# Four products that nobody reads behind each of the steps 8 to 26 of the recurrence

## The chip, the cores and the metric

The kernel runs on one core of a Trainium2 chip. A core has five engines that work side by side, each through a queue of its own in a fixed order: TensorE (PE in the profile; PEld is its loading of weights), VectorE (DVE), ScalarE (ACT), GpSimd (POOL) and SyncE (SP), which here issues nearly all DMA transfers. TensorE writes into PSUM, eight banks of 128 x 512 floats; VectorE and ScalarE read them out. Engines wait for one another by semaphores. The metric is the device time of one execution in microseconds (us), the median of several runs. [...]

## The reference

Two layers of a streaming encoder on 256 tokens of width 2048, all in float32. Layer 0 mixes tokens by causal pooling, layer 1 by RWKV-7; a SwiGLU block with a hidden width of 5632 follows each. The part that matters is the recurrence of layer 1, for 32 heads of size 64:

```python
def step(state, inp):
    r_t, w_t, k_t, v_t, a_t, b_t = inp
    sa = jnp.einsum('bhvk,bhk->bhv', state, a_t)
    state = (state * w_t[:, :, None, :] + sa[..., None] * b_t[:, :, None, :]
             + v_t[..., None] * k_t[:, :, None, :])
    return state, jnp.einsum('bhvk,bhk->bhv', state, r_t)
...
_, y = lax.scan(step, state0, seq_in)
...
return (y * g) @ w_o
```

## The kernel before, in words

Every float32 product of a large matrix is made of three products of a shorter float format (fp32r): ScalarE rounds a weight tile (`wh`, line 152), VectorE takes the rest (`wl`, line 153), and TensorE multiplies both. The stages follow one another: the pooling layer, the SwiGLU block (`ffn`, lines 311 to 347), the RWKV layer (`rwkv`), the second SwiGLU block.

The recurrence isn't stepped token by token. The 256 tokens are cut into four chunks of 64, and the 32 heads into eight groups of four (`gi`). For each group `ready(gi)` loads two tiles `KB` and `AR` that an earlier stage has put into DRAM (lines 832, 833), transposes them (L840), multiplies them (L853), masks the result into `G` (VectorE, L856), and completes the inverse of a small triangular system `Z` (L875, L882). `chains(gi)` then goes through the four chunks, three steps each, 12 steps for a group. A step is a few small float32 products of 64 or 128 rows and a copy out of PSUM: L907 and L910 into `cb`, then ScalarE's copy `rhs` (L912); L916, then the copy into `vt` or `sv` (L917); L921 and L925, then VectorE's update of the state `S` (L930, L932) and ScalarE's `Se` and `y` (L936, L937). A new group begins every 8 steps (`STAG`), so that one or two groups are under way; `all_chains` counts 68 steps in all.

`weave` puts the other work of this stage between the steps: `invert(1)` inverts the systems of groups 4 to 7 by 31 rounds of two VectorE instructions (`sysP`, L633, and `sysZ`, L634) on a tile `sysM` that four DMAs load (L624) out of `dM`, which the last of the `prepare` steps has written (L607); `head_norm` normalises a finished group (ScalarE's `ysq` L980 and a square root L990, VectorE's L976 to L996), where a DMA L973 brings a row of weights into a place that the group before must have left; `gating` (L958 to L960) multiplies `hid` by a loaded tile; `out_proj` (L1022 to L1024) multiplies finished groups by the output weights with 512 columns a product.

The program names the work in this order, and a scheduler sorts it by priorities (the chains' are raised) and by when it thinks that operands are there; the order on each engine is fixed when the program is built. PSUM banks come from three pools: three for `acc`, three for `g` (`g_bank`, used by `ready`, `head_norm`, `gating` and, until it ends, `prepare`), two for `cb`. A bank is given out in rotation and is waited for until its last reader is done. `queued(name)` keeps an instruction behind another on the same engine.

Of the kernel before, what the change touches and what calls it, by code (L numbers as in the profile page):

```python
# [40 lines left out]
LASTO = 6  # L41
OA, OB = 0, 0
STAG, OG, RE = 8, 2, 0
BANKS = {"acc": 3, "g": 3, "cb": 2}
DECAY = float(np.exp(-0.5))

# [46 lines left out]
def hybrid_encoder(ctx: ExitStack, tc: tile.TileContext, I, out):  # L93
    nc = tc.nc
# [5 lines left out]
    base = cp.tile([128, 5120], F32, name="base")  # L100
# [34 lines left out]
    last = {}  # L135

    def queued(name):
        return tc.issue_after(last[name].ins)
# [111 lines left out]
    def ffn(layer, each=None):  # L250
        gcol = par[f"g2_{layer}"]
        with ExitStack() as st:
# [1 line left out]
            ff = st.enter_context(tc.tile_pool(name="ff", bufs=1))  # L254
            tps = st.enter_context(tc.tile_pool(name="ftp", bufs=1, space=PSUM))
            ps = st.enter_context(tc.tile_pool(name="fps", bufs=1, space=PSUM))
            rb = base[:, 4864:]
            xs = []
            xs_ = ff.tile([128, KT * 512], F32R, name="xs")
            for k in range(KT):  # L260
# [189 lines left out]
    def rwkv():  # L450
        with ExitStack() as st:
# [3 lines left out]
            def mx(dt, name="mx"):  # L455
                return lp.tile([128, 512], dt, name=name, tag="mx", bufs=MX)
# [23 lines left out]
            hid = [hid_[:, q * 512:(q + 1) * 512] for q in range(4)]  # L480
# [16 lines left out]
            def bank(tag, bufs):  # L497
                return ps[tag].tile([128, 512], F32, name=tag, tag=tag, bufs=bufs)

            acc_bank = lambda: bank("acc", BANKS["acc"])  # L500
            g_bank = lambda: bank("g", BANKS["g"])
            cb_bank = lambda: bank("cb", BANKS["cb"])

# [383 lines left out]
            def chains(gi):  # L887

                vt, z, S = vts[gi], Z[gi % 3], Sb[gi % 2]
                ar_, kbt_, g_ = AR[gi], KBT[gi], G[gi]  # L890
                y = ys_raw[gi] = mx(F32, "y")

                sv = (vt, c2.tile([128, 512], F32, name="sv", tag="sv", bufs=3))
                nc.gpsimd.tensor_copy(sv[1][kh[1]], vt[kh[1]])
                odd[gi] = sv[1]
                heads_ = [(jj, slice(hd * 64, hd * 64 + 64), jj * 2 + hd) for jj in range(2) for hd in range(2)]
                Se = None
                for c in range(4):
                    q, i = c % 2, c // 2
                    k_, b_ = kh[q], kh[1 - q]  # L900
                    vrow = sv[q][:, i * 256:(i + 1) * 256]
                    rows_of = lambda u: vrow[:, u * 64:(u + 1) * 64]
                    two = lambda x: x.rearrange("p (j c) -> p j c", j=2)
                    with tc.high_priority(HP):
                        cb = cb_bank().rearrange("p (j x c) -> p j x c", j=2, x=2)
                        for jj, hc, u in heads_:
                            nc.tensor.matmul(cb[:, jj, 0, hc], lhsT=g_[jj][u % 2][k_, c], rhs=rows_of(u)[k_], start=(u == 0), stop=False, skip_group_check=True)  # L907
                        if c:
                            for jj in range(2):
                                nc.tensor.matmul(cb[:, jj, 0], lhsT=ar_[jj][:, c], rhs=S[c % 2][:, jj], start=False, stop=False, skip_group_check=True)  # L910
                        rhs = c2.tile([128, 2, 128], F32, name="rhs", tag="rhs", bufs=2)
                        nc.scalar.copy(rhs[b_], cb[b_, :, 0])  # L912
                    yield
                    with tc.high_priority(HP):
                        for jj, hc, u in heads_:
                            nc.tensor.matmul(cb[b_, jj, 1, hc], lhsT=z[b_, u * 2 + i], rhs=rhs[b_, jj, hc], start=True, stop=True, skip_group_check=True)  # L916
                        nc.scalar.copy(two(vrow[b_]), cb[b_, :, 1])  # L917
                    yield
                    with tc.high_priority(HP):
                        for jj, hc, u in heads_:  # L920
                            nc.tensor.matmul(cb[k_, jj, 0, hc], lhsT=g_[jj][u % 2][b_, c, k_], rhs=rows_of(u)[b_], start=False, stop=True, skip_group_check=True)  # L921
                        if c < 3:
                            up = cb[:, :, 1]
                            for jj, hc, u in heads_:
                                nc.tensor.matmul(up[hc, jj, :64], lhsT=kbt_[jj][:, c, hc], rhs=rows_of(u), start=True, stop=True, skip_group_check=True)  # L925
                            S2 = S[1 - c % 2]
                            for jj, hc, u in heads_:
                                e_ = ends[hc, gi * 2 + jj, c:c + 1]
                                if c:
                                    nc.vector.scalar_tensor_tensor(S2[hc, jj, hc], up[hc, jj, :64], e_, Se[hc, jj, hc], ALU.mult, ALU.add)  # L930
                                else:
                                    nc.vector.tensor_scalar(S2[hc, jj, hc], up[hc, jj, :64], e_, None, ALU.mult)  # L932
                            if c < 2:
                                Se = c2.tile([128, 2, 128], F32, name="Se", tag="Se", bufs=2)
                                for jj in range(2):
                                    nc.scalar.activation(Se[:, jj], S2[:, jj], AF.Copy, scale=ends[:, gi * 2 + jj, c + 1:c + 2])  # L936
                        nc.scalar.copy(two(y[k_, i * 256:(i + 1) * 256]), cb[k_, :, 0])  # L937
                    yield

            def all_chains():  # L940

                live = []
                for step in range(7 * STAG + 12):
                    if step % STAG == 0 and step < 8 * STAG:
                        live.append(chains(step // STAG))
                    live = [g for g in live if next(g, g) is not g]
                    yield

            def gating(gi):
# [132 lines left out]
            E_ = 7 * STAG + 12  # L1082
            more += [(last_weights(), 4, E_ - 12, E_ - 2), (head_norm(7, 0, 1), 4, E_ - 5, E_)]
            weave(all_chains(), *more)
            outs = chained(*rest)
            for _ in head_norm(7, 1, 2):
# [5 lines left out]

    pool_layer()
    ffn(0)
    rwkv()
    if True:
        def times_gain(n, fgB):
            with queued("load"):
                nc.sync.dma_start(fgB, I["rows"][3, n * 512:(n + 1) * 512].partition_broadcast(128))
            for i in range(2):  # L1100
                nc.vector.tensor_mul(h[i][n], h[i][n], fgB)

        ffn(1, times_gain)
        rstd = rstd_of_h()
        for n in range(4):
            for i in range(2):
                o = h[i][n]
                if i:
                    nc.scalar.activation(o, o, AF.Copy, scale=rstd[:, i:i + 1])
                else:  # L1110
                    nc.vector.tensor_scalar(o, o, rstd[:, i:i + 1], None, ALU.mult)
                (nc.sync if i else nc.scalar).dma_start(out[i * 128:(i + 1) * 128, n * 512:(n + 1) * 512], o)
# [53 lines left out]
```

## Time and profile before

| what | value |
|---|---|
| median of 3 runs | 2181.81 us (2181.44 to 2184.13) |
| the profiled execution, its own time | 2181.9 us |
| its span, first to last instruction | 2180.1 us |
| TensorE busy | 2116.9 us, 97% of the span |
| TensorE's weight loads busy | 1843.5 us, 85% |
| VectorE busy | 1553.9 us, 71% |
| ScalarE busy | 1147.3 us, 53% |
| mean granted TensorE clock | 0.981 |

A busy share is an average over all stages. The row of the clock cuts the span into 40 slices of 54.5 us. In a timeline a row is one instruction or a run of like ones: its start, how long it took, and in brackets how long its engine had stood idle before it and who ended that. The matmuls of a run overlap, so their pace is read from one start to the next. A float32 matmul of the program appears in the trace as two.

### The profile page before, as it was taken

To read this page: it belongs to the slowest core of one execution; us is meant where nothing else is said; L and a number is where in the kernel's file an instruction comes from. 1 tells how busy PE (TensorE), PEld (TensorE's weight loads), DVE (VectorE), ACT (ScalarE), POOL (GpSimd) and SP (SyncE) were. 2 spreads that over 40 slices of the span, in tenths; PEclk is the share of its full clock that TensorE was granted. 3 is DMA by queue.
4 is the path that set the end of the run, shared out by engine and by line. 5 is a ranking of instruction groups with operands and counts; after the bars stand their busy time and mean duration, and the time that the engine had idled before them with its cause. 6 is when DMAs were issued, how large, how long until landed. Compare 5 with 4: busy or idle time off the path is not lost.

```text
span 2180.1 us, 34748 instructions
## 1 busy us (share of the span) xinstructions
PE 2116.9 (97%) x13318; PEld 1843.5 (85%) x13318; DVE 1553.9 (71%) x2548; ACT 1147.3 (53%) x1884; POOL 30.6 (1%) x72
## 2 busy tenths in 40 slices
PE   7999999999999989999999999999999999999997
PEld 5888888888878879999988778788888888888786
DVE  8666666666787978688866767876666666677886
ACT  5544444444555478766745354554444444445444
POOL 0000000000000000011000000000000000000000
PEclk9999999999999999999998699999999999999999
DMA  6555565665566645466565343446666666655654
GB/s 232 174 187 191 186 191 187 190 187 190 196 198 217 207 155 163 163 210 207 171 218 151 108 121 105 160 121 191 188 189 189 188 189 189 188 191 199 204 202 156
DMA packets 147478, 395.11 MB, mean 181 GB/s; under 512 B 39280, under 2 KB 46832, under 8 KB 147056
## 3 DMA queue, kind: packets, MB, share of 16 engines
q1 hardware_dynamic: 146160, 390.80, 56.2%
q8 instruction: 104, 1.70, 0.3%
q10 hardware_dynamic: 1152, 2.10, 0.3%
q14 instruction: 62, 0.51, 0.1%
HBM read 376.59 MB, written 16.25 MB: 180 GB/s over the span
## 4 chain that ended last, share of the span: by engine, by line
PE 86%; DVE 6%; DMA 4%; ACT 2%; issue 1%; SPq 0%; ACTq 0%; DVEq 0%
PE acc L311 29%; PE acc L347 17%; PE acc L313 15%; PE acc L691 2%; PE acc L689 2%; PE acc L690 2%; DVE wl L153 2%; PE tp L347 2%; PE acc L1022 1%; PE acc L1024 1%; PE acc L1023 1%; DMA raw<-in_w 1%; PE acc L516 1%; PE acc L515 1%; PE cb L907 1%
## 5 line engine op out<-in xcount | busy, mean ns | idle before, releaser
L153 DVE TENSOR_TENSOR wl<-raw,wh 128x1024 fp32r<-128x1024 f32 (+1 forms) x525 | 640.2, 1220 | 432.2 <-ACT wh L152 428.0
L152 ACT CAST wh<-raw 128x1024 fp32r<-128x1024 f32 (+1 forms) x525 | 548.5, 1045 | 648.7 <-PE acc L311 276.9
L311 PE MATMUL acc<-xs,wh 128*128 128x512 f32 x2816 | 710.6, 393 | 3.7 <-DVE xs L266 3.2
L311 PEld LDWEIGHTS acc<-xs,wh 128*128 128x128 f32 x2816 | 504.9, 189 | 94.9 <-DVE xs L266 5.1
L313 PEld LDWEIGHTS acc<-xs,wl 128*128 128x128 f32 x2816 | 384.1, 190 | 27.5
L313 PE MATMUL acc<-xs,wl 128*128 128x256 f32 x2816 | 392.7, 282 | 0.0
L347 PE MATMUL acc<-vh,gT 128*128 128x512 f32 x640 | 184.9, 390 | 0.8 <-ACT vh L152 0.8
L347 PEld LDWEIGHTS acc<-vh,gT 128*128 128x128 f32 x640 | 119.7, 188 | 27.3 <-ACT vh L152 2.6
L691 PE MATMUL acc<-mx,wl 128*128 128x256 f32 x464 | 133.0, 287 | 3.5 <-DVE wl L153 3.5
L689 PE MATMUL acc<-mx,wh 128*128 128x256 f32 x464 | 132.1, 285 | 0.0
L690 PE MATMUL acc<-mx,wh 128*128 128x256 f32 x464 | 131.8, 284 | 0.0
L153 DVE TENSOR_TENSOR vl<-raw,vh 128x1024 fp32r<-128x1024 f32 x80 | 95.5, 1221 | 27.1 <-ACT vh L152 19.7
L347 PE MATMUL acc<-vl,gT 128*128 128x512 f32 x320 | 112.2, 389 | 0.0
L152 ACT CAST vh<-raw 128x1024 fp32r<-128x1024 f32 x80 | 80.9, 1050 | 49.3 <-PE acc L347 22.7
L355 ACT CAST vh<-T 128x1024 fp32r<-128x1024 f32 x56 | 58.9, 1052 | 80.5 <-DVE T L397 43.6
L347 PE MATMUL acc<-wh,gT 128*128 128x512 f32 x320 | 93.8, 390 | 0.7 <-ACT wh L152 0.7
L691 PEld LDWEIGHTS acc<-mx,wl 128*128 128x128 f32 x464 | 88.5, 191 | 5.3 <-DVE wl L153 5.2
L689 PEld LDWEIGHTS acc<-mx,wh 128*128 128x128 f32 x464 | 88.5, 191 | 0.8
L690 PEld LDWEIGHTS acc<-mx,wh 128*128 128x128 f32 x464 | 88.6, 191 | 0.0
L347 PE MATMUL acc<-vh,g 128*128 128x512 f32 x280 | 77.9, 391 | 1.1 <-ACT vh L355 0.6
L516 PE MATMUL acc<-wl,mx 128*128 128x256 f32 x256 | 74.2, 290 | 1.2 <-DVE wl L153 1.1
L515 PE MATMUL acc<-wh,mx 128*128 128x256 f32 x256 | 74.2, 290 | 0.0
(329 smaller groups left out, 3118.5 us busy)
## 6 DMA issues: line engine op xcount, KB each, us to landing
raw<-in_w SPq DMA_DIRECT2D x528, 512.0 KB, 4.4
raw<-in_wk SPq DMA_DIRECT2D x32, 512.0 KB, 3.7
raw<-in_wr SPq DMA_DIRECT2D x32, 512.0 KB, 3.7
raw<-in_wv SPq DMA_DIRECT2D x32, 512.0 KB, 4.0
raw<-in_wo SPq DMA_DIRECT2D x32, 512.0 KB, 3.6
raw<-in_pw SPq DMA_DIRECT2D x8, 512.0 KB, 7.8
dKB<-KB SPq DMA_DIRECT2D x16, 256.0 KB, 3.1
dKB<-AR SPq DMA_DIRECT2D x16, 256.0 KB, 3.7
```

Source lines behind the costliest of these rows:

```text
L152: nc.scalar.copy(wh[:P, :step], raw[:P, :step])
L153: nc.vector.tensor_sub(wl[:P, :step], raw[:P, :step], wh[:P, :step].bitcast(F32))
L311: nc.tensor.matmul(acc, lhsT=w[:, cs], rhs=xs[q * 4 + kk], start=(q + kk == 0), stop=False, skip_group_check=True)
L313: nc.tensor.matmul(acc[:, :256], lhsT=l[:, cs], rhs=xs[q * 4 + kk][:, :256], start=False, stop=(q + kk == 6), skip_group_check=True)
L347: nc.tensor.matmul(out_, lhsT=lhsT, rhs=rhs, start=start, stop=stop, skip_group_check=True)
L355: nc.scalar.copy(wh, src)
L515: nc.tensor.matmul(av[:, i], lhsT=xh, rhs=w[:, cs], start=(k == 0 and i == 0), stop=False, skip_group_check=True)
L516: nc.tensor.matmul(av[:, i], lhsT=xh, rhs=l[:, cs], start=False, stop=False, skip_group_check=True)
L689: nc.tensor.matmul(acc[:, :256], lhsT=w[:, cs], rhs=xs[k][:, :256], start=(k == 0), stop=False)
L690: nc.tensor.matmul(acc[:, :256], lhsT=w[:, cs], rhs=xs[k][:, 256:], start=False, stop=False)
L691: nc.tensor.matmul(acc[:, :256], lhsT=l[:, cs], rhs=xs[k][:, :256], start=False, stop=(k == 15))
L907: nc.tensor.matmul(cb[:, jj, 0, hc], lhsT=g_[jj][u % 2][k_, c], rhs=rows_of(u)[k_], start=(u == 0), stop=False, skip_group_check=True)
```

## The change

`idle_products` takes a bank of the `g` pool and multiplies four times a 128 x 128 part of `hid[2]` by the 512 columns of `hid[3]` into it. Nothing reads the bank. `all_chains` calls it once behind each of the steps 8 to 26, 19 times, so that 76 products come in. Each is queued behind the last of the chains' L907, L916 or L921 that stands before it in the program. The slice of `base` in `ffn` names its end now; the tile has that width anyway.

```diff
+IDLE0, IDLE1, IDLES = 8, 27, 4
...
-            rb = base[:, 4864:]
+            rb = base[:, 4864:5120]
...
-                            nc.tensor.matmul(cb[:, jj, 0, hc], lhsT=g_[jj][u % 2][k_, c], rhs=rows_of(u)[k_], ...)
+                            last["chain"] = nc.tensor.matmul(cb[:, jj, 0, hc], lhsT=g_[jj][u % 2][k_, c], rhs=rows_of(u)[k_], ...)
...
+            def idle_products():
+
+                acc = g_bank()
+                for _ in range(IDLES):
+                    with queued("chain"):
+                        nc.tensor.matmul(acc, lhsT=hid[2][:, :128], rhs=hid[3], start=True, stop=True, skip_group_check=True)
+
             def all_chains():
...
                     live = [g for g in live if next(g, g) is not g]
+                    if IDLE0 <= step < IDLE1:
+                        idle_products()
                     yield
```

The scheduler sorts the whole stage anew. Line numbers grow by 1 from line 44 on and by 10 behind `idle_products`. On TensorE the order ahead of the first new product is the old one, and so is that behind the end of the RWKV layer; in between much has changed its place.

Three places follow. The first is TensorE at the first new products, in `ready` of group 2: `KB_12332` is the first `KB` tile of that group and `KB_12460` the second (in the new program `KB_12337` and `KB_12475`). Before:

```order
L853 MATMUL g_12405<-AR_12333,KB_12332 128x128 x4
L907 MATMUL cb_12521<-sv_12321,base_64 128x64 x4
L910 MATMUL cb_12521<-S_11276,AR_11800 128x128
L910 MATMUL cb_12521<-S_11276,AR_11952 128x128
L853 MATMUL g_12406<-AR_12333,KB_12332 128x128 x4
L907 MATMUL cb_12687<-vt_10845,base_64 128x64 x4
L840 MATMUL g_12465<-base_64,KB_12460 128x128 x4
L853 MATMUL g_12547<-AR_12461,KB_12460 128x128 x2
L916 MATMUL cb_12521<-rhs_12528,Z1_11271 64x64 x4
```

Now, where L946 is the new product:

```order
L946 MATMUL g_12410<-hid_6918 128x512 x4
L854 MATMUL g_12415<-AR_12338,KB_12337 128x128 x4
L854 MATMUL g_12416<-AR_12338,KB_12337 128x128 x4
L908 MATMUL cb_12717<-vt_10845,base_64 128x64
L917 MATMUL cb_12536<-rhs_12543,Z1_11271 64x64
L946 MATMUL g_12470<-hid_6918 128x512 x4
L917 MATMUL cb_12536<-rhs_12543,Z1_11271 64x64 x3
L908 MATMUL cb_12717<-vt_10845,base_64 128x64 x3
L841 MATMUL g_12480<-base_64,KB_12475 128x128 x4
L946 MATMUL g_12545<-hid_6918 128x512 x4
L946 MATMUL g_12567<-hid_6918 128x512 x4
L922 MATMUL cb_12536<-sv_12321,base_64 64x64 x4
```

Three groups of four stand ahead of the transposes of the second `KB` tile, two right behind them, and the chain's L916 has moved ahead of these transposes.

The second place is SP's queue at the same time, with the loads of the second `KB` tile of group 2 (`dKB5`), of `sysM`, and of the next group's first `KB` tile (`dKB6`). Before:

```order
L832 DMA KB_12460<-dKB5_6925 128x512
L833 DMA AR_12461<-dKB5_6925 128x512
L1066 DMA base_64<-dH01_6943 128x512
L1066 DMA base_64<-dH02_6944 128x512
L624 DMA sysM_12374<-dM1_6937 32x32x32 x4
L1066 DMA base_64<-dH03_6945 128x512
L869 DMA m12_12804<-dM0_6936 32x8x32 x2
L973 DMA base_64<-in_rows 128x256
L832 DMA KB_12805<-dKB6_6926 128x512
L833 DMA AR_12806<-dKB6_6926 128x512
```

Now:

```order
L1076 DMA base_64<-dH01_6943 128x512
L625 DMA sysM_12379<-dM1_6937 32x32x32 x3
L833 DMA KB_12475<-dKB5_6925 128x512
L625 DMA sysM_12379<-dM1_6937 32x32x32
L834 DMA AR_12476<-dKB5_6925 128x512
L1076 DMA base_64<-dH02_6944 128x512
L1076 DMA base_64<-dH03_6945 128x512
L870 DMA m12_12849<-dM0_6936 32x8x32 x2
L833 DMA KB_12850<-dKB6_6926 128x512
L834 DMA AR_12851<-dKB6_6926 128x512
L983 DMA base_64<-in_rows 128x256
```

The loads of `dKB5` have moved behind three and four of the `sysM` loads, and those of `dKB6` ahead of the row of `head_norm`.

The third place is ScalarE's queue, with the copy `sv_12321` that the chain of group 1 needs and the square `ysq` of `head_norm(0)`. Before:

```order
L912 COPY rhs_12528<-cb_12521 64x256
L844 ACTIVATE KBT_12464<-g_12465,misc_6904 128x2x128 x2
L980 ACTIVATE ysq_12565<-y_11787 128x512
L917 COPY sv_12321<-cb_12521 64x256
L990 ACT_TABLE_LOAD
```

Now:

```order
L913 COPY rhs_12543<-cb_12536 64x256
L918 COPY sv_12321<-cb_12536 64x256
L845 ACTIVATE KBT_12479<-g_12480,misc_6904 128x2x128 x2
L990 ACTIVATE ysq_12590<-y_11787 128x512
L1000 ACT_TABLE_LOAD
```

The copy `sv` has moved from behind the square to a place ahead of it.

## Rows read from the trace of the kernel before

**Rows 1.** The page, 40 slices of the span: granted TensorE clock in tenths
```profile
PEclk9999999999999999999998699999999999999999
```

**Rows 2.** Stretches: length, busy PE, PEld, DVE, ACT, POOL (instructions), PEclk, DMA share, GB/s
```profile
1105.00:1183.51 78.51, 77.63 (x837) 69.84 (x836) 52.87 (x110) 44.18 (x98) 7.21 (x17) 1.00 0.59 187
1183.51:1217.64 34.13, 28.24 (x204) 23.31 (x202) 26.17 (x73) 10.63 (x25) 0.76 (x1) 0.50 0.26 71
1234.71:1251.78 17.07, 16.69 (x92) 13.73 (x91) 7.23 (x18) 5.45 (x13) 0.00 (x0) 0.50 0.39 110
1282.49:1289.32 6.83, 6.16 (x16) 4.55 (x16) 1.84 (x3) 0.85 (x3) 0.00 (x0) 0.50 0.87 248
1176.30:1252.46 76.16, 67.90 (x541) 56.26 (x540) 51.11 (x138) 28.44 (x68) 1.87 (x3) 0.66 0.40 115
1188.29:1233.00 44.71, 39.93 (x347) 33.14 (x347) 38.47 (x111) 18.27 (x43) 0.76 (x1) 0.67 0.26 81
```

**Rows 3.** Timeline, TensorE, waits and what stood behind: start, us, line, tiles, [idle before]
```profile
...
1181.54 0.66 PE L840 MATMUL g<-base,KB 128*128 128x128 f32 x4 [0.79 <-DMA KB<-dKB]
...
1190.29 1.11 PE L921 MATMUL cb<-sv,base 64*64 64x64 f32 x8 [4.01 <-ACT sv L917]
...
1192.41 0.58 PE L958 MATMUL g<-hid,lbh 128*128 128x256 f32 x1
...
1201.51 1.11 PE L840 MATMUL g<-base,KB 128*128 128x128 f32 x4 [1.88 <-DMA KB<-dKB]
...
```

**Rows 4.** Timeline, TensorE: like work at both levels of the clock
```profile
...
1208.46 3.09 PE L853 MATMUL g<-AR,KB 64*128 64x128 f32 x16
...
1212.50 0.63 PE L1022 MATMUL acc<-wh,ys 128*128 128x512 f32 x1
1212.92 0.63 PE L1023 MATMUL acc<-wl,ys 128*128 128x512 f32 x1
...
1249.15 0.77 PE L1023 MATMUL acc<-wl,ys 128*128 128x512 f32 x1
...
1255.25 1.16 PE L853 MATMUL g<-AR,KB 64*128 64x128 f32 x16
...
1264.28 0.39 PE L1022 MATMUL acc<-wh,ys 128*128 128x512 f32 x1
1264.51 0.39 PE L1023 MATMUL acc<-wl,ys 128*128 128x512 f32 x1
...
```

**Rows 5.** Timeline, ScalarE, around the wait of 4.01 us
```profile
...
1189.35 0.63 ACT L980 ACTIVATE ysq<-y 128x512 f32<-128x512 f32 x1 [6.22 <-DVE sysZ L634]
1189.88 0.35 ACT L917 COPY sv<-cb 64x256 f32<-64x256 f32 x1
...
```

**Rows 6.** Timeline, SP, issues of the loads
```profile
...
1176.77 0.45 SPq L832 DMA_DIRECT2D KB<-dKB  x1
...
1179.34 6.73 SPq L624 DMA_DIRECT2D sysM<-dM  x4
...
1197.22 0.35 SPq L973 DMA_DIRECT2D base<-in_rows  x1
1197.61 0.44 SPq L832 DMA_DIRECT2D KB<-dKB  x1
...
```

**Rows 7.** Timeline, VectorE, the inversion and its longest idle times
```profile
...
1188.29 0.21 DVE L633 TENSOR_TENSOR sysP<-sysM,sysZ 128x31 f32<-128x31 f32 x1 [7.32 <-DMA sysM<-dM]
...
1223.61 0.69 DVE L856 TENSOR_TENSOR G<-g,misc 128x512 f32<-128x512 f32 x1 [1.21 <-PE g L853]
...
1229.34 0.28 DVE L930 SCALAR_TENSOR_TENSOR S<-cb,misc,Se 64x64 f32<-64x64 f32 x1 [1.15 <-PE cb L925]
...
1232.82 0.19 DVE L634 TENSOR_TENSOR sysZ<-sysZ,sysP 128x31 f32<-128x31 f32 x1
...
```

**Rows 8.** Timeline, TensorE, around 1282.5 us
```profile
...
1281.44 0.68 PE L916 MATMUL cb<-rhs,Z 64*64 64x64 f32 x8 [0.46 <-ACT rhs L912]
1283.16 0.80 PE L1022 MATMUL acc<-wh,ys 128*128 128x512 f32 x1 [1.04 <-DVE G L856]
...
```

More of the change, by code (lines that the diff above doesn't have):

```diff
@@ L906, in chains @@
                         for jj, hc, u in heads_:
-                            nc.tensor.matmul(cb[:, jj, 0, hc], lhsT=g_[jj][u % 2][k_, c], rhs=rows_of(u)[k_], start=(u == 0), stop=False, skip_group_check=True)
+                            last["chain"] = nc.tensor.matmul(cb[:, jj, 0, hc], lhsT=g_[jj][u % 2][k_, c], rhs=rows_of(u)[k_], start=(u == 0), stop=False, skip_group_check=True)
                         if c:
@@ L915, in chains @@
                         for jj, hc, u in heads_:
-                            nc.tensor.matmul(cb[b_, jj, 1, hc], lhsT=z[b_, u * 2 + i], rhs=rhs[b_, jj, hc], start=True, stop=True, skip_group_check=True)
+                            last["chain"] = nc.tensor.matmul(cb[b_, jj, 1, hc], lhsT=z[b_, u * 2 + i], rhs=rhs[b_, jj, hc], start=True, stop=True, skip_group_check=True)
                         nc.scalar.copy(two(vrow[b_]), cb[b_, :, 1])
@@ L920, in chains @@
                         for jj, hc, u in heads_:
-                            nc.tensor.matmul(cb[k_, jj, 0, hc], lhsT=g_[jj][u % 2][b_, c, k_], rhs=rows_of(u)[b_], start=False, stop=True, skip_group_check=True)
+                            last["chain"] = nc.tensor.matmul(cb[k_, jj, 0, hc], lhsT=g_[jj][u % 2][b_, c, k_], rhs=rows_of(u)[b_], start=False, stop=True, skip_group_check=True)
                         if c < 3:
```

## The prediction

> **What bounds the kernel now.** I began with the page's slices, because the change adds TensorE work in one short part of the program. TensorE's clock is at the upper level nearly throughout; it is lower only in the 24th and 25th slice, in the recurrence [rows 1]. The stretches show where [rows 2]: up to 1183.51 us it is 1.00, then it is 0.50 for 34.13 us, again for 17.07 us from 1234.71 on, and for 6.83 us from 1282.49 on, 1.00 between them. The first two lie inside the steps that get the products. The timeline puts the first new group (it now stands ahead of the transposes of the first tile of group 2) at 1176.30 us and the last ahead of the out-projection that ends in the chain's L907 at 1252.46; that is a stretch of 76.16 us, with TensorE busy for 67.90 us of it at a mean clock of 0.66 [rows 2]. I call it the stretch. It is also the only place where TensorE's order changes much.
>
> What sets the pace in it changes twice. At first it is a transfer: VectorE waits 7.32 us for `sysM` [rows 7], and meanwhile TensorE stands still for 4.01 us for the copy `sv` [rows 3], which ScalarE holds behind the square `ysq`, itself waiting for 6.22 us [rows 5]. Then VectorE works through the inversion, 38.47 us of 44.71 us busy until 1233 us [rows 2]; its longest waits there are for TensorE, 1.21 and 1.15 us [rows 7]. Behind the inversion it is TensorE alone: 16.69 of 17.07 us busy at half clock, while VectorE is busy for 7.23 us [rows 2]. Behind the stretch TensorE is the bound again, so what is won or lost by 1252.46 should stay until the end.
>
> What half clock costs is read from like work at both levels [rows 4]. The 16 matmuls of L853 from 1208.46 on take 3.09 us, those from 1255.25 on 1.16 us. Products of 128 x 512 follow one another after 0.42 us at half clock (1212.50, 1212.92) and after 0.23 us at full clock (1264.28, 1264.51). That is a ratio of 1.8 for the products and of 2.7 for the small ones. I take a factor of 1.9, near the products, because most of TensorE's time in these stretches is in columns of that kind.
>
> **The change part by part.** The slice in `ffn` is the same slice and costs nothing. There remain the products and the new order.
>
> *The products.* They have the form of the last rows, 128 x 128 by 512 columns, so 76 x 0.23 = 17.5 us at full clock, and 76 x 0.42 = 31.9 us if all of them ran at half. Nothing hides them but waits of TensorE, and a product can't fill a wait that begins behind it. The trace shows this with other work: L958 needs only `hid` and a tile loaded long before, yet it starts at 1192.41, behind L921 that had waited 4.01 us [rows 3]. So I charge all 17.5 us. [...]
>
> *The clock.* If the products keep it up, the work that ran at half clock shrinks: 28.24 + 16.69 = 44.93 us busy [rows 2] become 44.93 / 1.9 = 23.6 us, that is -21.3 us.
>
> *A new stretch at half clock.* The clock fell behind short waits: after 0.79 us and thin work at 1183.5 [rows 3], after 0.46 and 1.04 us at 1282.5 [rows 8]. A longer wait comes now. The second `KB` tile was issued at 1176.77, ahead of the `sysM` loads, whose issue took 6.73 us from 1179.34 on [rows 6]. Now it stands behind three of the four, so I put its issue at about 1184 (estimate). From issue to first use it took 4.8 us before (1176.77 to 1181.54), the next one 3.9 us (1197.61 to 1201.51) [rows 3, 6]; so it lands at about 1188. Ahead of it TensorE has its old work from 1176.30 on, 1181.54 - 0.79 - 1176.30 = 4.45 us [rows 3], L916 with 0.7 us [rows 8] and twelve products with 2.8 us, so it stands still from about 1184.2 on, some 3.9 us. There the clock will fall as it did before. Each return in the trace stands behind a run of 512-column products: back at 1217.64 with such a run from 1212 on, back at 1251.78 with one from 1249.15 on [rows 2, 4]. Eight new products stand right behind the wait, 8 x 0.42 = 3.4 us, and four more soon after. So I expect the clock back at about 1196, 8 us after 1188, half of which is lost: +4 us. The ends are +2 us (back at 1192) and +15 us (back only at 1217.6 as before, 29.6 / 2).
>
> *The waits.* TensorE idles 76.16 - 67.90 = 8.26 us in the stretch [rows 2]. Of these the 4.01 us go, because `sv` stands ahead of the square now; what is late next on ScalarE is the square itself, which only `head_norm` needs. The 1.88 us at 1201.51 [rows 3] go too: that tile was issued at 1197.61, behind the row of `head_norm` issued at 1197.22, which had to wait for its place [rows 6], and now it is issued ahead of it. The 0.79 us become the 3.9 us above. That leaves 8.26 - 4.01 - 1.88 - 0.79 + 3.9 = 5.5 us, or -2.8 us.
>
> *VectorE's own bound.* Its inversion can't begin earlier, since `sysM` comes when it came. With 38.47 us of work in 44.71 us it could end 6.2 us earlier at most. Behind it TensorE's 16.69 us become 8.8, less about 12 products (2.8 us): 5.1 us. Together no more than 11.3 us can be won in the stretch; the sum for TensorE lies above that, so TensorE decides.
>
> *The later half-clock stretch.* It costs 6.16 - 6.16 / 1.9 = 2.9 us. No product stands there, but the order does change: the two waits ahead of it [rows 8] come from a copy of ScalarE and a mask of VectorE that met TensorE at that moment. I take them not to meet again: -2.9 us.
>
> **The sum**: 17.5 - 21.3 + 4.0 - 2.8 - 2.9 = -5.5 us, from 2181.9 us of the profiled execution (2180.1 us of span and 1.8 us around it, 0.1 us above the median of the runs) to 2176.4 us.
>
> **The rivals.** *The later stretch stays.* Its cause lies outside the steps with products, and in the old trace the clock held or fell by waits of a microsecond. For it: nothing in the change reaches 1282 us directly. Against: the order around it is new. Then 17.5 - 21.3 + 4.0 - 2.8 = -2.6 us: 2179.3 us, no change that can be told.
>
> *The products run at half clock themselves.* The wait for the second `KB` tile drops the clock; when the eight products behind it are too few and the next ones come one group at a time between small float32 matmuls, it stays down until the out-projection, about 1217.6 as before. Then +15 in place of +4, and the waits at 1282 come again: -5.5 + 11 + 2.9 = +8.4 us, 2190.3 us. For it: between 1192 and 1212 the old program ran whole rows of L958 and L853 without the clock coming back. Against: no row of 512 columns stood among those. The point from which it decides: a return later than about 1207 eats the gain (19 us at half clock cost 9.5 us), with the later stretch still there 1202. [...]
>
> *The clock holds throughout and no wait is left*, VectorE's bound: -11.3 - 2.9 = -14.2 us, 2167.7 us. I count it into the forecast as its lower end.
>
> That the products aren't issued where they are meant to be is no rival: the order shows 19 groups of four between the chain's rows.
>
> **How the numbers follow.** Forecast 0.47, the later stretch stays 0.27, half clock 0.26. A change under 0.2% (4.4 us, 2177.4 to 2186.2) can't be told from none. The forecast lies below it, the first rival inside, the second mostly above; so faster 0.47, same 0.27, slower 0.26. The likeliest's own range is 2168 to 2179 us. The range of 8 in 10 goes from the lower bound to the price of half clock: 2168 to 2190 us.
>
> **What would show it.** In the changed profile the stretch from the first product to the L907 behind the last lasts about 73.5 us. The clock falls once, near 1187, for less than 12 us, and not again at 1234 nor at 1282. The wait of L921 for `sv` and that of the first transposes of group 3 are gone; one of about 4 us for the second `KB` tile has come. The products follow one another after 0.23 us. VectorE's last `sysZ` ends between 1229 and 1234 us. I am wrong if the clock comes back only past 1207, if the transposes of the second `KB` tile wait over 8 us, if VectorE's inversion starts later than 1190, or if TensorE waits for banks between the products.

## The result and the profile after

The change made the kernel slower: 2196.39 us, median of 4 runs (2191.4 to 2200.21), against 2182.97 us (2181.44 to 2185.43) for the kernel before on the same chip. The ratio is 1.0055, with an interval of 1.0032 to 1.0079. In a second set it was 1.0077 (1.0053 to 1.0102). The forecast was 2176.4 us, with 2168 to 2190 as its range; the sign is wrong too.

The profiled execution took 2191.4 us, with a span of 2189.6 us and a mean granted clock of 0.990 (before: 0.981). It is the fastest of the four; the mean clock of ten runs of the changed kernel is 0.9864. So a higher clock and a longer time stand together. The page's slices of the clock, which answer to [rows 1]:

```profile
PEclk9999999999999999999999999999999999999999
```

The dip of the 24th and 25th slice is gone. The stretches of the new kernel, with the columns of [rows 2]:

```profile
1175.43:1245.37 69.94, 68.95 (x623) 55.41 (x622) 49.49 (x137) 28.96 (x68) 1.72 (x3) 0.98 0.46 126
1185.98:1189.39 3.41, 3.41 (x15) 2.36 (x13) 2.63 (x9) 2.57 (x5) 0.00 (x0) 0.50 0.42 130
1245.37:1428.01 182.64, 178.45 (x1419) 143.60 (x1418) 122.61 (x251) 84.77 (x178) 1.84 (x3) 0.93 0.37 113
1254.24:1257.66 3.42, 3.42 (x20) 3.26 (x19) 1.82 (x5) 1.82 (x4) 0.00 (x0) 0.50 0.42 153
1291.79:1298.62 6.83, 6.83 (x41) 6.00 (x40) 3.78 (x13) 4.14 (x9) 0.61 (x1) 0.50 0.02 4
1360.06:1366.88 6.82, 6.82 (x35) 5.20 (x34) 4.28 (x13) 3.19 (x8) 0.00 (x0) 0.50 0.01 2
1414.67:1421.50 6.83, 4.54 (x19) 4.37 (x20) 4.98 (x16) 1.75 (x4) 0.00 (x0) 0.50 0.35 108
```

The first row is the prediction's stretch, from the first product to the chain's row behind the last. It has shrunk from 76.09 us (1176.30 to 1252.39, where that row begins in the trace of before; the prediction has 1252.46) to 69.94 us although it holds 76 matmuls more, and its clock has risen from 0.66 to 0.98. The third row runs on from there to a matmul that both programs have at the end of the last projection. Before, that part was this row, the same columns:

```profile
1252.39:1417.50 165.11, 161.53 (x1423) 130.82 (x1423) 122.61 (x250) 84.60 (x177) 1.84 (x3) 0.98 0.41 128
```

The matmuls are the same but for records that the traces miss, VectorE's work is equal to the hundredth, and yet the part is 17.5 us longer. Its clock is 0.93 in place of 0.98, from the four stretches at half clock (0.50) that are listed last above; before it held one, 6.83 us long [rows 2]. So -6.15 us were won in the stretch and 17.5 us lost behind it; all the rest is 1.9 us shorter (0.87 ahead of the first product, 1.0 at the end). The sum is the 9.5 us between the two profiled executions.

Two of the three waits of [rows 3] went as forecast. TensorE's timeline of the new kernel, at the second `KB` tile, at the chain's L922 that once waited for `sv`, and at group 3's first `KB` tile:

```profile
1184.94 0.63 PE L841 MATMUL g<-base,KB 128*128 128x128 f32 x4 [0.99 <-DMA KB<-dKB]
1185.32 3.21 PE L946 MATMUL g<-hid 128*128 128x512 f32 x8
1188.46 1.08 PE L922 MATMUL cb<-sv,base 64*64 64x64 f32 x8
...
1199.39 2.13 PE L946 MATMUL g<-hid 128*128 128x512 f32 x8
1201.35 0.60 PE L841 MATMUL g<-base,KB 128*128 128x128 f32 x4
```

No wait is left at L922 nor at 1201.35. SP, ScalarE and VectorE at the same place (rows of [rows 5 to 7] in the new order):

```profile
1176.71 4.21 SPq L625 DMA_DIRECT2D sysM<-dM  x3
1181.02 0.51 SPq L833 DMA_DIRECT2D KB<-dKB  x1
```

```profile
1183.18 0.37 ACT L918 COPY sv<-cb 64x256 f32<-64x256 f32 x1 [4.07 <-PE cb L917]
1186.33 0.63 ACT L990 ACTIVATE ysq<-y 128x512 f32<-128x512 f32 x1
```

```profile
1185.17 0.20 DVE L634 TENSOR_TENSOR sysP<-sysM,sysZ 128x31 f32<-128x31 f32 x1 [3.12 <-DMA sysM<-dM]
1232.13 0.19 DVE L635 TENSOR_TENSOR sysZ<-sysZ,sysP 128x31 f32<-128x31 f32 x1
```

The tile `KB` was issued at 1181.02 us, 3 us earlier than estimated, and the wait for it was 0.99 us, not 3.9. VectorE began its inversion at 1185.17, 3.1 us earlier than before, and ended it at 1232.13, inside the forecast's 1229 to 1234.

What the same matmuls do behind the stretch is seen where a chain's step meets `ready`. TensorE's timeline of the kernel before, two places:

```profile
1255.25 1.16 PE L853 MATMUL g<-AR,KB 64*128 64x128 f32 x16
1256.34 0.27 PE L916 MATMUL cb<-rhs,Z 64*64 64x64 f32 x1
1256.36 0.27 PE L921 MATMUL cb<-sv,G 64*64 64x64 f32 x1
1256.45 0.22 PE L916 MATMUL cb<-rhs,Z 64*64 64x64 f32 x1
1256.46 0.22 PE L921 MATMUL cb<-sv,G 64*64 64x64 f32 x1
...
1257.02 0.69 PE L875 MATMUL g<-w,m 32*32 32x32 f32 x32
1257.64 0.50 PE L1022 MATMUL acc<-wh,ys 128*128 128x512 f32 x1
...
1260.07 1.10 PE L907 MATMUL cb<-vt,G 64*128 64x64 f32 x8
1261.10 0.67 PE L921 MATMUL cb<-sv,G 64*64 64x64 f32 x8
```

And of the changed kernel, with the same steps of another group:

```profile
1250.64 0.37 PE L876 MATMUL g<-w,m 32*32 32x32 f32 x10
1250.94 0.43 PE L908 MATMUL cb<-vt,G 64*128 64x64 f32 x2
1251.30 0.24 PE L876 MATMUL g<-w,m 32*32 32x32 f32 x2
1251.48 0.43 PE L908 MATMUL cb<-vt,G 64*128 64x64 f32 x2
1251.84 0.24 PE L876 MATMUL g<-w,m 32*32 32x32 f32 x2
1252.01 0.43 PE L908 MATMUL cb<-vt,G 64*128 64x64 f32 x2
1252.37 0.24 PE L876 MATMUL g<-w,m 32*32 32x32 f32 x2
1252.55 0.43 PE L908 MATMUL cb<-vt,G 64*128 64x64 f32 x2
1252.91 0.38 PE L876 MATMUL g<-w,m 32*32 32x32 f32 x12
1253.21 0.68 PE L922 MATMUL cb<-sv,G 64*64 64x64 f32 x8
```

Before, 32 matmuls of 32 x 32 in one run took 0.62 us (1257.02 to 1257.64) and eight of L907 1.03 us. Now 28 and eight of them, cut into one another, take 2.57 us (1250.64 to 1253.21), at full clock and with no wait. Two costs are in this. Going from one tile size to another costs about 0.1 us: worked out from one start to the next at full clock in the trace of before, a 128x512 matmul takes 0.231 us ahead of one of its own tile size and 0.326 ahead of another's, a 64x64 one 0.058 and 0.148. And some small matmuls overlap where they are neighbours in the order: at 1256.34 L916 and L921, of two chains, start 0.01 to 0.02 us apart, in place of the 0.058 of 64x64 matmuls behind their own kind.

With each TensorE step counted from one start to the next, its idle time taken off and its form's mean at full clock as the price, the 17.5 us come out as: 187 changes of tile size in place of 137, +4.8 us; what is left at full clock, +5.8, where the same matmuls stand less often side by side; half clock, +6.4 (9.1 us lost in place of 2.8); idle, +0.6. Another choice of prices moves single terms by 1 to 2 us.

### The profile page after: what moved, and what is told of

Read it like the earlier page. It is cut to its first block, busy times and chain, and to the rows that moved or that the text cites. A ratio compares the mean times of both kernels' runs of the same rounds, so it can differ in the third digit from the quotient of the medians.

```text
span 2189.6 us, 34909 instructions
## 1 busy us (share of the span) xinstructions
PE 2133.4 (97%) x13394; PEld 1854.2 (85%) x13394; DVE 1552.4 (71%) x2548; ACT 1148.1 (52%) x1884; POOL 30.4 (1%) x72
## 4 chain that ended last, share of the span: by engine, by line
PE 89%; DVE 4%; DMA 3%; ACT 2%; issue 1%; SPq 0%; ACTq 0%; DVEq 0%
PE acc L312 29%; PE acc L348 18%; PE acc L314 15%; PE acc L692 2%; PE acc L690 2%; PE acc L691 2%; DVE wl L154 2%; PE tp L348 2%; PE cb L908 2%; PE acc L1032 1%; PE acc L1033 1%; PE acc L1034 1%; PE g L854 1%; PE acc L516 1%; PE acc L517 1%
```

## The experiments

Each run gives its time and its mean granted clock, and the scatter of one kernel's runs is mostly that clock: over 211 runs of the twelve kernels, before and the changed one among them, 0.001 of mean clock goes with 1.75 us, and taking it out lowers the spread within a kernel (standard deviation) from 5.0 to 2.0 us. "At equal clock" below is a kernel's mean after that much is taken off, minus that of the kernel before (85 runs, mean clock 0.9811). It is a fit, uncertain by 1 to 2 us. The runs come from two chips. At equal clock the kernel before is 1.5 us faster on the chip of after_again, order_only, products_only and waits_out than on that of the other kernels, so a difference between kernels of the two chips carries that too.

| kernel | median us (runs) | ratio (95%) | clock | at equal clock |
|---|---|---|---|---|
| after_again | 2200.15 (6) | 1.0077 (1.0053 to 1.0102) | 0.9864 (10 runs of both sets) | +22.7 |
| order_only | 2193.26 (7) | 1.0054 (1.0030 to 1.0078) | 0.9816 | +9.8 |
| products_only | 2187.77 (12) | 1.0019 (1.0003 to 1.0034) | 0.9897 | +17.3 |
| waits_out | 2175.70 (12) | 0.9978 (0.9960 to 0.9995) | 0.9834 | -3.2 |
| bank_only | 2188.45 (11) | 1.0030 (1.0011 to 1.0049) | 0.9807 | +5.4 |
| gram_split | 2183.95 (11) | 1.0006 (0.9984 to 1.0027) | 0.9823 | +3.4 |
| hold_late | 2170.93 (5) | 0.9942 (0.9920 to 0.9963) | 0.9871 (17 of both) | -0.3 |
| hold_late_again | 2174.43 (12) | 0.9946 (0.9926 to 0.9967) | | |
| hold_both | 2174.84 (10) | 0.9952 (0.9933 to 0.9972) | 0.9903 | +6.7 |
| more_switches | 2190.99 (12) | 1.0027 (1.0003 to 1.0050) | 0.9803 | +5.7 |
| hold_tiny | 2178.83 (12) | 0.9972 (0.9948 to 0.9996) | 0.9828 | -1.8 |
| hold_one | 2175.91 (12) | 0.9962 (0.9941 to 0.9982) | 0.9852 | -1.3 |

Most of these kernels pin the order: a table of ranks, written at the end of the program, ties each engine's instructions into one list. Their diffs below are then changes of that list, in the line numbers of the kernel before.

```diff
+    for e, at in ORDER.items():
+        for a, b in zip(at, at[1:]):
+            tc.add_manual_dep(rows[e][b], rows[e][a].name, NoSync, reason="order")
```

No run pins the order of before and changes nothing else, so what the table costs by itself is not measured.

**after_again**: the changed kernel once more, beside the next two.

> The changed kernel once more, beside the others of this set. In its first profile it lost 11.4 us against before between 1176 and 1428 us: half clock and waits gave back 12.0 and 6.7 us, the products took 20.6, and 10 us more went into the same matmuls as before, in another order. Theory 'order' and theory 'products' both expect 2191 to 2200 us, about 1.0055 of before.

It was 1.0077 of before, as above. Its profiled execution lost only 5.4 us to half clock in the whole stage, against 10.6 in the first one; so one trace of a kernel is one draw of its clock, and only the means of many runs are set against each other below.

**order_only**: the kernel before without any product, every engine in the order of the changed kernel.

```diff
 # ORDER: that of the changed kernel, its products left out
-idle_products()
```

> The kernel before, with no products, but every engine's instructions stand in the changed kernel's order. Theory 'order': the loss comes with the new order, which has 50 more changes of tile size on TensorE (0.09 us each, 4.6 us) and does the two heads' gram matmuls of a pair one after the other instead of side by side (some 7 us), against 6.7 us of waits that it loses; so about 2182.9 + 4.6 + 7 - 6.7 = 2188 us if as much runs at half clock as before, and between 2183 and 2195. Theory 'products': the loss is the products' own, and the order without them is only better by its waits, about 2176 us.

The order alone costs as much by its ratio as the whole change: 1.0054, at the clock of before, +9.8 us. In its stage TensorE changes tile size 265 times in place of 215, and the same matmuls at full clock take 234.6 us in place of 222.7, some 12 us more. Its idle time falls only from 11.8 to 10.6 us; with the products in, it was 5.2. Two of its stretches, columns as before:

```profile
1182.49:1196.14 13.65, 11.25 (x88) 9.94 (x88) 10.10 (x34) 5.21 (x11) 0.00 (x0) 0.50 0.50 136
1226.86:1240.51 13.65, 13.52 (x74) 11.27 (x73) 7.47 (x21) 5.56 (x11) 0.00 (x0) 0.50 0.46 124
```

Without products the clock falls in both places of before again, for shorter. And it falls four times behind the stretch, where the changed kernel does:

```profile
1250.75:1254.17 3.42, 3.42 (x26) 3.23 (x25) 2.13 (x6) 1.36 (x3) 0.00 (x0) 0.50 0.45 153
1288.30:1295.13 6.83, 6.83 (x46) 5.98 (x47) 3.21 (x12) 3.68 (x9) 0.00 (x0) 0.50 0.01 2
1356.57:1363.39 6.82, 6.82 (x35) 5.41 (x35) 4.05 (x13) 3.31 (x8) 0.00 (x0) 0.50 0.01 2
1411.18:1418.01 6.83, 4.49 (x20) 4.30 (x20) 5.07 (x16) 1.76 (x4) 0.00 (x0) 0.50 0.34 105
```

Each stands 3.5 us ahead of its counterpart there (1254.24, 1291.79, 1360.06, 1414.67), so these four falls come with the new order and need no product. after_again shows three of them, at 1254.81, 1295.77 and 1415.23.

**products_only**: the order of before, with the 19 groups of four put right behind the chain's rows.

```diff
 L907 MATMUL cb<-vt,base x4
+MATMUL g<-hid 128x512 x4
 L840 MATMUL g<-base,KB x4
```

> The 76 products, but all other instructions of every engine stand in the order of the kernel before; each group of four stands right behind the chain's matmuls that it was queued behind (some a few matmuls later, where a bank is free). Theory 'order': the products cost 76 x 0.23 us and 18 more changes of tile size at 0.09 us, 19.2 us together, and give back 12 to 20 us of half clock; the old waits stay. So 2182.9 + 19.2 - 16 = 2186 us (2182 to 2190), less than the changed kernel by 8 to 12 us. Theory 'products': as slow as the changed kernel or slower, 2196 us and more.

At equal clock the 76 products cost 17.3 us; the prediction's 76 x 0.23 was 17.5. The clock gave back (0.9897 - 0.9811) x 1750 = 15 us of it. That left the ratio at 1.0019, inside the range of theory 'order' and well under the 2196 us of theory 'products'. That clock isn't full: in the profiled execution it fell among the products, and four groups ran at half clock (four products in 2.07 us, in place of 1.20):

```profile
1202.40:1226.29 23.89, 23.77 (x105) 17.81 (x106) 17.48 (x44) 5.97 (x16) 0.61 (x1) 0.50 0.24 75
```

**waits_out**: of the new order only the two moves that take waits away.

```diff
 L912 COPY rhs
+L917 COPY sv
 L844 ACTIVATE KBT x2
 L980 ACTIVATE ysq
-L917 COPY sv
...
+L832 DMA KB<-dKB6
+L833 DMA AR<-dKB6
 L973 DMA base<-in_rows
-L832 DMA KB<-dKB6
-L833 DMA AR<-dKB6
```

> The kernel before with two pieces of the new order alone: ScalarE copies sv ahead of the square ysq, and SP issues the loads of KB and AR of group 3 ahead of the row of head_norm. TensorE's order is that of before. If the waits were worth what the trace of before says, 4.0 and 1.9 us go: 2176 to 2179 us, ratio 0.997 to 0.998. Rival: the next wait on the path (sysM, 7.3 us of VectorE) or a clock that falls elsewhere takes their place: 2182 to 2184 us.

It is faster than before, by 3.2 us at equal clock; idle time fell by 4.3 us (11.8 to 7.6), not by the 5.9 of the two waits, because TensorE now waits 2.49 us for VectorE's `S` at 1197.04. The mean clock is a little higher (0.9834), but both stretches are still there.

```profile
1186.04:1216.76 30.72, 28.15 (x202) 23.36 (x202) 25.15 (x71) 10.74 (x25) 0.76 (x1) 0.50 0.32 80
1233.82:1250.89 17.07, 16.37 (x92) 13.53 (x91) 7.30 (x18) 5.78 (x13) 0.00 (x0) 0.50 0.37 103
```

**bank_only**: what makes the order new. The changed kernel with one product of 8 columns in place of four of 512; the scheduler sorts for itself.

```diff
-IDLE0, IDLE1, IDLES = 8, 27, 4
+IDLE0, IDLE1, IDLES = 8, 27, 1
...
-                        nc.tensor.matmul(acc, lhsT=hid[2][:, :128], rhs=hid[3], ...)
+                        nc.tensor.matmul(acc[:, :8], lhsT=hid[2][:, :128], rhs=hid[3][:, :8], ...)
```

> The changed kernel with one product of 8 columns in place of each four of 512: 19 tiny products, which take 19 banks of pool g at the same places, and the scheduler sorts it by itself. Theory 'bank': the new order comes from the banks, which a pool hands out in the order of the program, so that the small matmuls behind a product can't run ahead of it; the order changes as much as in the changed kernel (42 more changes of tile size than before, against 50), with no clock held up, so as slow as the new order alone: 2188 to 2195 us. Rival: the order moved because the scheduler reckoned with the time of the products; then these 19 move little, and the time is that of before, 2180 to 2184 us.

It has next to no work and still a new order: 263 changes of tile size by its trace, in place of 215. So a bank and a place in the queue are enough to reorder the stage. The price at equal clock, +5.4 us, is about half that of order_only; the two together are shown to be a cause, not to be the whole of it, and no run tells the bank from the place in the queue.

**gram_split**: one suspected cost of the order by itself. In all 12 pairs of heads the second head's four matmuls of L853 stand behind the first head's, in the same slots.

```diff
-L853 head 0, head 1, head 0, head 1, ...
+L853 head 0 x4, head 1 x4
```

> The kernel before, but in the 12 pairs of gram matmuls of the stages ready(2) to ready(7) the four of the second head stand behind the four of the first, in the same slots of TensorE's order; nothing else moves. Theory 'side by side': heads that alternate run on two halves of the array at once; 16 records then take 1.09 us, and 2 x 1.09 us when apart. 7 to 8 of the 12 pairs alternate before, so 8 to 10 us more: 2189 to 2193 us. Rival: the pace of these matmuls is set by something else (their tile size, the loads), and the time stays at 2180 to 2184 us.

The effect is there. Its timeline, and its 192 matmuls grouped (busy us, mean ns):

```profile
1258.35 1.71 PE L876 MATMUL g<-AR,KB 64*128 64x128 f32 x16
...
L876 PE MATMUL g<-AR,KB 64*128 64x128 f32 x192 | 27.0, 318 | 0.0
```

Sixteen of them take 1.71 us in place of 1.16 [rows 4]. The same group of the kernel before was busy for 4.6 us less:

```profile
L853 PE MATMUL g<-AR,KB 64*128 64x128 f32 x192 | 22.4, 324 | 0.1
```

By the program the two heads read different halves of the partitions, and in these traces they overlap as long as they alternate; what in TensorE brings that about no run shows. The ratio, 1.0006, can't be told from 1: at equal clock it is +3.4 us, and a slightly higher clock (0.9823) hid it. The size was half of what was expected: a pair of heads costs 0.55 us more when apart, not 1.09, and 7 to 8 pairs make 4 us.

**more_switches**: the other suspected cost. At 21 places behind 1255 us the last out-projection matmul of a run stands in the middle of the chain's next four matmuls, which makes 42 more changes of tile size.

```diff
-L1022 MATMUL acc 128x512
 L916 MATMUL cb 64x64 x4
+L1022 MATMUL acc 128x512
 L916 MATMUL cb 64x64 x4
```

> The kernel before, but at 21 places behind 1255 us the last out-projection matmul of a run stands in the middle of the chain's four 64-row matmuls that follow it, which makes 42 more changes of tile size on TensorE and changes nothing else. Theory 'changes of tile size': each costs 0.09 us, as the pace in the traces says; 42 x 0.092 = 3.9 us more at the same clock: 2185 to 2188 us, ratio about 1.0018, with the clock of before. Rival: the 0.09 us at a change overlaps with something that is waited for anyway, and the time stays within 1 us.

42 x 0.094 = 3.9 us would be expected; it was +5.7 us (by 1.6 us uncertain) at equal clock. What TensorE does at a change no run shows, only the time that it takes.

**hold_late**: few products at the right place. waits_out, and three groups of four products just ahead of the two waits that waits_out has left there (at 1232.27 and 1235.70 us in its trace) and of the next matmuls of L853.

```diff
+MATMUL g<-hid 128x512 x4
 L916 MATMUL cb<-rhs,Z x8
```

> The kernel with the two waits taken out (2175.7 us), and three groups of four products, 12 in all, ahead of TensorE's waits at about 1231 and 1235 us and ahead of the gram matmuls at 1241 us, where the clock fell before; the order of all else is kept. If products hold the clock through a thin place: the half-clock stretch of 17 us from 1234 on goes (-7 us), 12 x 0.23 us and 0.5 us for changes of tile size come, of which 1.6 us lie in waits: 2169 to 2172 us. Rival: the clock falls all the same, and the products cost 2 to 3 us: 2177 to 2180 us.

0.9942 of before: faster than both kernels. The same part of the stage, where waits_out ran at half clock for 17.07 us:

```profile
1229.00:1250.00 21.00, 20.92 (x213) 16.95 (x212) 13.61 (x28) 11.50 (x25) 0.61 (x1) 1.00 0.50 138
```

Against waits_out it costs 2.9 us at equal clock (12 x 0.23 = 2.8, but the two ran on different chips) and gains 0.0037 of clock, 6.5 us.

**hold_both**: hold_late and four groups more in the early stretch, 16 products.

```diff
+MATMUL g<-hid 128x512 x4   (at about 1182, 1190, 1193 and 1198 us)
```

> As the last one, with four more groups (16 products) at about 1182, 1190, 1193 and 1198 us, to hold the clock through the inversion too. There VectorE is busy for nearly the whole time, so a held clock is worth little: half of the 31 us at half clock goes at best, and what that gives back is bounded by VectorE's idle time of some 3 to 6 us, against 16 x 0.23 + 0.7 = 4.4 us less what lies in waits: 2168 to 2174 us, no better than the last one. Rival: TensorE sets the pace there too, and the held clock is worth 10 us more: 2160 to 2166 us.

The clock rose to 0.9903, and no gain came of it: 0.9952. At equal clock it is 7.0 us above hold_late, where the products account for 3.7. I take the rest for VectorE's inversion, which sets the pace there whatever TensorE's clock. One pair of traces agrees: from its first `sysP` to its last `sysZ` it takes 41 us in hold_both (1190.56 to 1231.62) and in hold_late (1187.61 to 1228.59), though TensorE is at half clock for 10 us of it in the one and for 21 in the other. A wait has also come back in hold_both, because ScalarE's `KBT` ahead of `sv` now waits 10.60 us, by the profile for VectorE:

```profile
1191.61 0.84 ACT L884 ACTIVATE KBT<-g,misc 128x256 f32<-128x256 f32 x2 [10.60 <-DVE sysZ L674]
1192.75 1.11 PE L961 MATMUL cb<-sv,base 64*64 64x64 f32 x8 [4.47 <-ACT sv L957]
```

In hold_late `KBT` began 0.85 us behind its transposes (1180.91, 1181.76), here 7.6 us (1183.99, 1191.61). Only the added products differ; whether it is the banks that they take was not tested. In the same execution the clock fell at 1229.43, ahead of the first of the three late groups, and these, which hold_late ran in 1.20 us each, took 2.07. So the three late groups hold the clock in two of the three traces that have them, not in every execution.

**hold_tiny**, **hold_one** and **hold_late_again**: is it the columns? hold_late with 8 columns a product, with one product of 512 a group, and unchanged.

```diff
-MATMUL g<-hid 128x512 x4
+MATMUL g<-hid 128x8 x4     (hold_tiny)
+MATMUL g<-hid 128x512 x1   (hold_one)
```

> The kernel hold_late, whose 12 products take 8 columns instead of 512, at the same places and in the same banks. If it is the products' work that keeps the clock up, it falls at 1234 us as without them: 2175 to 2179 us and a clock of about 0.983. Rival: the gain of hold_late came from its banks or from a lucky clock; then this one is as fast, 2169 to 2172 us.

> hold_late with one product per group in place of four, 3 in all, 0.7 us. Theory: the clock is held by how much TensorE has done just before, and three products are too few: 2175 to 2178 us with the clock of the kernel without waits (0.983). Rival: one each is enough at a place that is just too thin: 2167 to 2170 us.

> hold_late once more, beside its two variants: 2169 to 2173 us, 0.994 to 0.995 of before, and a clock of 0.988 to 0.990.

With 8 columns the fall is back, and the ratio (0.9972) is that of waits_out. hold_tiny's stretch:

```profile
1229.72:1250.20 20.48, 20.48 (x107) 16.70 (x105) 8.67 (x20) 6.43 (x14) 0.00 (x0) 0.50 0.33 88
```

With three products the profiled run falls too, somewhat earlier, and the mean clock over all runs lies between (0.9852):

```profile
1226.66:1243.73 17.07, 16.97 (x92) 13.04 (x93) 10.22 (x29) 8.51 (x19) 0.00 (x0) 0.50 0.46 130
```

hold_late came out the same again, 0.9946, and its profile has no fall at 1234 either. So by these runs it is the work in the products that holds the clock, not the order or the banks that they take: at the same places and in the same banks the mean clock is 0.9871 with four products of 512 columns a group and 0.9828 with four of 8; waits_out, without any, has 0.9834.

## Why the prediction was wrong

**Inside the stretch it held, and was too cautious.** Forecast: 73.5 us; measured: 69.94. Its terms, worked out as above: products 18.9 us (forecast 17.5); half clock -18.1 (forecast -21.3 + 4.0); waits -7.3, from 8.26 to 0.99 us (forecast -2.8); changes of tile size +0.4. The factor of half clock came out as 1.76 (44.92 us of work against 25.5 at full-clock prices), not 1.9. The 2.7 read from [rows 4] for small matmuls was not the clock's alone: the sixteen at 1208.46 stand for the most part head by head, those at 1255.25 alternate, and against gram_split's 1.71 us the 3.09 us are a factor of 1.8. The clock fell once, at 1185.98, a microsecond off the forecast, and came back after 3.41 us. That it fell there is in part luck: the wait that was to drop it was 0.99 us, not 3.9, and after_again has such a wait (0.88 us at 1187.9) without a fall. Not each return in the trace of before stands behind a run of 512-column products: the one at 794.39 us, after 10.24 us at half clock, stands behind matmuls of 128 and 256 columns. VectorE's inversion did begin earlier, against "Its inversion can't begin earlier", because three `sysM` loads now go ahead of `KB`. The rival that the clock stays down until the out-projection did not come true in this trace, though eight products ran mostly at half clock (3.21 us from 1185.32 on); in products_only four groups did, from 1202.40 on. No product of the changed kernel waited for a bank there: the only wait in the stretch is that of 0.99 us for `KB`.

**The step that failed** is the one behind the stretch: "what is won or lost by 1252.46 should stay until the end", with "It is also the only place where TensorE's order changes much". The front part of this document says that in between the first product and the end of the layer much has changed its place, and the prediction priced that new order at nothing, but for a gain of 2.9 us where "I take them not to meet again". What stood there was +17.5 us. Equal work did not mean equal time on TensorE: the neighbours of a matmul decided a part of its price. order_only shows that this needs no product: there the same matmuls at full clock take 234.6 us in place of 222.7.

**The sum, redone on means of runs.** The forecast at equal clock was 17.5 - 2.8 = +14.7 us, and -21.3 + 4.0 - 2.9 = -20.2 us by the clock. Measured: +22.7 and (0.9864 - 0.9811) x 1750 = -9.3, together +13.4. So the miss of 18.9 us has two halves: 8.0 us of work made dearer by its order, and 10.9 us of clock that did not come back. In the order of before the products return 15 us of clock, in the new one 9.3 (the difference is uncertain by 4 us). The later stretch did not go: it became four, and order_only has the same four without a product. Three of them (1254.24, 1291.79, 1360.06) have TensorE busy throughout. What it did ahead of the first is shown above, 32- and 64-row matmuls cut into one another without a wait; rows of the same kind stand ahead of the other two. That this thin work, which the new order makes, is what drops the clock fits, but no run took it away there.

**What is additive and what is not.** products_only and order_only sum to 27.1 us at equal clock, the change has 22.7: the products partly fill waits that the order alone still has (idle 10.6 us there, 5.2 in the changed kernel). The prediction charged all products in full because TensorE works in order, as L958 did behind the wait of 4.01 us [rows 3]; where they stand ahead of a wait, they do take its place.

**Why the order changed.** In the orders of TensorE shown ahead of the prediction the numbers of the `g` tiles rise from one first write to the next, before and now, as they would if the pool hands out its three banks in the order of the program; for the whole program no run here shows it. If so, a product's bank ties the small matmuls of `ready` that come behind it to the chain's step that the product is queued behind. bank_only bears this out in kind. How much of the price beyond bank_only's comes from the scheduler's own estimate of the products' time stays open.

## What to carry to other kernels

A change that adds an instruction to a scheduled program also adds an order: compare the built orders over the whole stage, count the changes of tile size and the small matmuls that lost their concurrent neighbour, and price them before anything is called free. Here work that only holds the clock paid in a few places, right ahead of the waits at which the trace shows the clock falling: 12 products there gave 0.9942 (0.9920 to 0.9963), 76 spread over the steps 1.0055 (1.0032 to 1.0079). Where runs scatter with the clock, take the clock out before a term of 5 us is read from one trace.

## What the runs showed of the hardware that was not expected

- Going to a matmul of another tile size costs 0.09 to 0.10 us for most forms (0.231 to 0.326 us for 128x512, 0.105 to 0.201 for 64x128, at full clock in the trace of before).
- Two heads' matmuls of L853, sixteen of them, take 1.16 us when they alternate (before) and 1.71 when they follow one another (gram_split).
- TensorE's clock fell with TensorE busy all the time: 6.83 of 6.83 us from 1291.79 on, and its timeline shows no wait in the 15 us ahead of it; order_only does the same at 1288.30.
- Twelve products of 512 columns kept the granted clock at 1.00 where waits_out ran at 0.50, in both profiles of hold_late but not in that of hold_both; twelve of 8 columns did not.
